# A decoder block's prologue reordered: the second token block's rows loaded ahead of the conditioning weights, and the later sums and low parts given to VectorE

## The chip, the cores and the metric

One core of a Trainium2 chip runs the whole block. The metric is the device time of one execution in microseconds. Engines are named as in the profile: PE (TensorE), DVE (VectorE), ACT (ScalarE), POOL (GpSimd) and SP (SyncE, which here only issues transfers).

## The reference

One layer on a sequence of 2048 tokens, width 1024, all in float32. A vector c gives six vectors of shift, scale and gate; the first two act on the normed tokens, and those go through one input projection:

```python
mod = jax.nn.silu(c) @ w_cond[l] + b_cond[l]
shift_m, scale_m, gate_m, shift_f, scale_f, gate_f = [
    m[:, None, :] for m in jnp.split(mod, N_MOD, axis=-1)]
h = rmsnorm(x, g_mix_pre[l]) * (1.0 + scale_m) + shift_m
proj = h @ w_in[l]
q, k, v, u = jnp.split(proj, [SB_WIDTH, 2 * SB_WIDTH, 3 * SB_WIDTH], axis=-1)
...
attn = stick_breaking_attention(to_heads(q), to_heads(k), to_heads(v))
pool = pooling_mixer(u, w_pool[l], pool_scale[l])
mix = jnp.concatenate([attn, pool], axis=-1) @ w_out[l]
x = x + gate_m * rmsnorm(mix, g_mix_post[l])
```

A SwiGLU feed-forward with its own shift, scale and gate follows. The change is in the prologue: the first two of the six vectors, and the first products of the input projection.

## The kernel before, in words

Every float32 matrix product is made of three products of rounded parts. A tensor is split into a high part (a copy rounded by ACT) and a low part (the tensor minus its high part); `split` (L57) does this, the low part on DVE or, in `chunk_split` (L455), on POOL. `mm3` (L65) multiplies high by high, high by low and low by high.

Tokens go in four blocks of 512 (tb 0 to 3), turned so that the 1024 features lie on partitions in 8 tiles k of 128. The input projection is cut into chunks of 128 columns (q, k, u chunks, each a 512 KB transfer by `chunk_load`, L446). A product of a chunk with a token block is 8 x 3 = 24 matmuls of 128x512.

The order on PE, ACT, DVE and POOL is the order in which the code records them; SP's order is the scheduler's. Eight transfers can be under way at a time: each issue waits for the landing of the eighth before it.

The prologue has to bring together three things before the first product: normed and turned token rows, shift and scale as columns, and a split chunk of w_in. Shift and scale are sums over the 1024 rows of w_cond, weighted with silu(c), 8 steps kc with 128 rows each. They are made in two halves of 512 columns, and each half feeds four of the 8 tiles k:

- Rows of tb 0 are loaded (`row_load`, L555) into `early_hi`, normed (`normed_rows`, L308: square with row sum on ACT, a power on POOL, a scaling on DVE) and turned by PE (`turn_rows`, L573) into `turned`.
- First half: `sums_load` (L585) brings each pair of steps in two 512 KB pieces, one for each part. Part 0 (shift) is summed by DVE into `acc0` (`cond_step`, L214); part 1 (scale) by PE, with one column of weights, into one row, which `row_end` (L603) turns into a column. `sums_end` (L610) turns `acc0` into a column by matmuls with ones, adds the biases, and gives `mods` (held in `sumsq`).
- Then `modulate0` (L638) makes high and low parts of the tokens' tiles 0 to 3, and `first_products` (L654) multiplies three chunks (0, 1 and "third") with them. Rows of tb 1 were loaded into `early_lo`; they are normed and scaled, and `turn1` (L648) turns and modulates their tiles 0 to 3.
- Second half: both parts are summed by DVE, in 512-column steps with two accumulators; `sums_end(1)`, then tiles 4 to 7 of both blocks, and the rest of the first products.
- The fourth chunk ("fourth", u) opens the regular loop (`pieces`, L459, woven with `rest_of_cond`, L294, which sums parts 2 to 5 on DVE). In it `gate_part` (L237) makes the gate's broadcast with two pairs of matmuls into banks of `z_ps`.

PSUM has eight banks, handed out in fixed cycles: `z_ps` (three), `t_ps` (two), `av_ps` (two), `mm_only` (one). Regular products alternate between `z_ps` and `mm_only`.

Of the kernel before, what the change touches and what calls it, by code (L numbers as in the profile page):

```python
# [17 lines left out]
P = 128  # L18
# [26 lines left out]
def block_kernel(ctx, tc, x, c, w_cond, b_cond, g_mix_pre, g_mix_post, w_in, w_pool,  # L45
# [58 lines left out]
    mods["am"], mods["bm"] = sumsq[:, 0:KC], sumsq[:, KC:]  # L104
# [91 lines left out]
    c_sb = cond.tile([P, KC], F32, tag="c", bufs=1, name="c_sb")  # L196
    nc.sync.dma_start(c_sb, c[0].rearrange("(p kc) -> p kc", p=P))
    vrows = cond.tile([P, P], F32, tag="vrows", bufs=1, name="vrows")
    nc.sync.dma_start(vrows[0:48, :], b_cond[0].rearrange("(r q) -> r q", q=P))
    nc.sync.dma_start(vrows[48:56, :], g_mix_pre[0].rearrange("(r q) -> r q", q=P))  # L200
    nc.sync.dma_start(vrows[56:64, :], g_ffn_pre[0].rearrange("(r q) -> r q", q=P))
    nc.sync.dma_start(vrows[64:68, :], pool_scale[0].rearrange("(r q) -> r q", q=P))
    nc.scalar.activation(cs, c_sb, AF.Sigmoid)
    nc.vector.tensor_tensor(cs, cs, c_sb, ALU.mult)
    tv = t_ps("tv")
    nc.tensor.transpose(tv[:, 0:68], vrows[0:68, :], ident[0:68, 0:68])
    nc.vector.tensor_copy(colv, tv[:, 0:68])
# [29 lines left out]
    def gate_part(acc, part, g_post, dst):  # L237
# [7 lines left out]
        for half in range(2):  # L245
            cols = slice(half * TB, (half + 1) * TB)
            ps = z_ps(f"gp{part}_{half}")
            nc.tensor.matmul(ps, ones_r, hi[:, cols], start=True, stop=False)
            nc.tensor.matmul(ps, ones_r, lo[:, cols], start=False, stop=True)
            nc.vector.tensor_tensor(g[:, cols], g[:, cols], ps, ALU.mult)  # L250
# [9 lines left out]

    def cond_sums(part, acc):
        for kc in range(KC):
            while ahead_wc and len(coming_wc) <= 3:
                p, k = ahead_wc.pop(0)
                coming_wc.append(cond_load(p, k, new_wc(f"wc{p}_{k}") if k < 6 else spare[:, k - 6]))
# [42 lines left out]
    def normed_rows(tb, j, xs=None):  # L308
# [11 lines left out]
        if tb == 1:  # L320
            return lambda: nc.scalar.mul(xs, xt, r) if j % 2 else nc.vector.tensor_scalar_mul(xs, xt, r)
# [133 lines left out]
    def chunk_split(c, part):  # L455
        ks = slice(2 * part, 2 * part + 2)
        split(c[1][:, ks, :], c[2][:, ks, :], c[0][:, ks, :], nc.gpsimd)
# [101 lines left out]

    ready = [row_load(0, j) for j in range(4)]  # L560
    for j in range(4):
        normed_rows(0, j, ready[j])
    acc0 = new_acc(0)
    sums = [z_ps("am")]
    row = cond.tile([1, TB], F32, tag="brow", bufs=1, name="am_row")
    acc1 = cond.tile([P, D], F32, tag="acc", bufs=2, name="acc1")
    by_tensor = (tuple(range(KC)), ())
    by_vector = [[kc for kc in range(KC) if kc not in r] for r in by_tensor]
    halves = [slice(half * TB, (half + 1) * TB) for half in range(2)]
# [3 lines left out]
    def turn_rows(j):  # L573
        for half in range(2):
# [5 lines left out]
            if half or j > 1:  # L580
# [4 lines left out]
    def sums_load(half, pair):  # L585
        two = wcs[:, pair]
        wc = cond.tile([P, 2, TB], F32, tag="wc", bufs=4, name=f"wc1_{half}_{pair}")
        nc.sync.dma_start(wc, wc_rows[:, 2 * pair:2 * pair + 2, D + half * TB:D + (half + 1) * TB])
        nc.sync.dma_start(two, wc_rows[:, 2 * pair:2 * pair + 2, halves[half]])
        return two, wc  # L590

    def sums_step(half, pair, two, wc):
        for kk in range(2):
            kc = 2 * pair + kk
            cond_step(acc0[:, halves[half]], kc, two[:, kk])
            if kc in by_vector[half]:
                cond_step(acc1[:, halves[half]], kc, wc[:, kk])
            else:
# [70 lines left out]
    for pair in range(4):  # L669
        turn_rows(pair)  # L670
# [1103 lines left out]
```

## Time and profile before

| | |
|---|---|
| median of 3 runs | 2265.72 us (2265.38 to 2267.29) |
| the profiled execution | 2265.84 us |
| its span | 2264.0 us |
| mean granted PE clock | 0.996 |
| PE busy | 2231.9 us (99%) |
| DVE, ACT, POOL busy | 72%, 52%, 57% |
| first product of the projection starts | 27.07 us |
| fourth chunk's first product starts | 76.41 us |

A row of the profile's order of time has start (us from the span's start), duration, engine, line, operation, output<-inputs, shapes, count of merged instructions, and in brackets the engine's idle time ahead of it with what ended it. A row of the table by stretches of time has the stretch, its length, busy time and count for PE, PEld (weight loads), DVE, ACT and POOL, then the granted clock, the share of the transfer engines, and GB/s. "SPq" is SP issuing a transfer.

### The profile page before, as it was taken

How to read it: one execution, taken by the hardware profiler on the slowest of the kernel's cores; microseconds unless marked ns; L12 is line 12 of the kernel's file. 1: busy time of each engine (PE TensorE's matmuls, PEld its weight loads, DVE VectorE, ACT ScalarE, POOL GpSimd, SP SyncE). 2: the span in 40 equal slices, each digit the busy share in tenths (PEclk: the TensorE clock that was granted, in tenths of full speed). 3: DMA queues.
4: the chain of work that ended last, by engine and by line, in shares of the span. 5: the costliest groups of instructions: out<-in, count | busy, mean ns of one | idle time of the engine just before them, and what ended most of it. 6: DMA issues, size and time to landing. Idle time of an engine off the chain costs nothing.

```text
span 2264.0 us, 33220 instructions
## 1 busy us (share of the span) xinstructions
PE 2231.9 (99%) x10589; PEld 1845.3 (82%) x10589; DVE 1628.4 (72%) x2213; ACT 1167.3 (52%) x2422; POOL 1298.2 (57%) x1606
## 2 busy tenths in 40 slices
PE   7999999999999999999999999999999999999998
PEld 5788888888888878887888888888888888888887
DVE  6884599999999966666656566777866565655566
ACT  5334589989989854453232323455533323334444
POOL 3652267787779955546777777321676665651003
PEclk9999999999999999999999999999999999999999
DMA  8885886634443456665444455777853333328654
GB/s 298 302 298 204 288 213 178 174 91 117 134 112 108 139 189 214 222 219 171 160 160 161 158 163 180 270 242 229 259 174 122 101 112 94 115 88 296 216 189 149
DMA packets 323979, 413.55 MB, mean 183 GB/s; under 512 B 20630, under 2 KB 189146, under 8 KB 323676
## 3 DMA queue, kind: packets, MB, share of 16 engines
q1 hardware_dynamic: 319340, 408.81, 56.2%
q10 hardware_dynamic: 4464, 2.62, 0.4%
q8 instruction: 83, 1.36, 0.3%
q14 instruction: 92, 0.75, 0.1%
HBM read 282.90 MB, written 128.45 MB: 182 GB/s over the span
## 4 chain that ended last, share of the span: by engine, by line
PE 88%; DVE 5%; ACT 3%; issue 2%; DMA 1%; POOL 1%; SPq 0%; DVEq 0%; ACTq 0%; POOLq 0%
PE wt L914 4%; PE t_g L69 3%; PE t_u L69 3%; PE t_g L70 3%; PE t_u L70 3%; PE t_u L71 3%; PE t_g L71 3%; PE dn0p L71 3%; PE dn0p L70 3%; PE dn0p L69 3%; PE dn1p L70 3%; PE dn1p L69 3%; PE dn1p L71 3%; PE b_g L69 3%; PE b_g L70 3%; PE b_g L71 3%
## 5 line engine op out<-in xcount | busy, mean ns | idle before, releaser
L903 POOL TENSOR_TENSOR w<-sg,pr 128x512 f32<-128x512 f32 (+2 forms) x320 | 307.1, 960 | 47.6 <-DVE pr L898 16.1
L1288 POOL TENSOR_TENSOR s<-s,cu 128x512 f32<-128x512 f32 x88 | 133.6, 1525 | 237.5 <-DVE cu L1287 142.6
L898 DVE TENSOR_TENSOR_SCAN pr<-pr,carry,begin 128x512 f32<-128x512 f32 x192 | 243.9, 1270 | 0.0
L882 ACT ACTIVATE sg<-z 128x512 f32<-128x512 f32 (+2 forms) x320 | 183.4, 573 | 50.6 <-PE z L880 40.7
L60 DVE TENSOR_TENSOR wtl<-wt,wth 128x512 fp32r<-128x512 f32 (+1 forms) x320 | 189.2, 592 | 17.9 <-ACT wth L59 16.0
L59 ACT CAST wth<-wt 128x512 fp32r<-128x512 f32 (+1 forms) x320 | 182.1, 571 | 12.1 <-PE wt L914 12.1
L884 ACT ACTIVATE pr<-z 128x512 f32<-128x512 f32 (+2 forms) x320 | 182.5, 570 | 0.0
L914 PE MATMUL wt<-ident,w 128*128 128x128 f32 x1088 | 172.5, 273 | 1.8 <-POOL pr L894 1.1
L60 DVE TENSOR_TENSOR u_s_l<-u_s,u_s_h 128x512 fp32r<-128x512 f32 x66 | 65.2, 988 | 149.9 <-ACT u_s_h L59 149.9
L914 PEld LDWEIGHTS wt<-ident,w 128*128 128x128 f32 x1088 | 134.1, 140 | 33.2 <-POOL pr L894 1.9
L1278 ACT ACTIVATE s<-s 128x512 f32<-128x512 f32 x88 | 55.7, 633 | 184.7 <-DVE s L1277 184.7
L929 PE MATMUL av<-wth,vt 128*128 128x512 f32 (+1 forms) x320 | 126.4, 395 | 0.9 <-ACT o L934 0.8
L60 DVE TENSOR_TENSOR u_a_l<-u,u_a_h 128x512 fp32r<-128x512 f32 x66 | 76.2, 1156 | 63.6 <-ACT u_a_h L59 63.6
L930 PE MATMUL av<-wtl,vt 128*128 128x512 f32 (+1 forms) x320 | 118.1, 369 | 1.9 <-DVE wtl L60 1.7
L69 PE MATMUL dn0p<-w0p_h,g0p_h 128*128 128x512 f32 x308 | 119.8, 389 | 0.0
L70 PE MATMUL dn0p<-w0p_l,g0p_h 128*128 128x512 f32 x308 | 119.8, 389 | 0.0
L71 PE MATMUL dn0p<-w0p_h,g0p_l 128*128 128x512 f32 x308 | 119.8, 389 | 0.0
L879 PE MATMUL z<-kt,qt 128*128 128x512 f32 (+2 forms) x320 | 118.7, 371 | 0.7 <-ACT pr L884 0.6
L59 ACT CAST g_s_h<-g_s 128x512 fp32r<-128x512 f32 x66 | 39.5, 620 | 152.5 <-POOL g_s L1220 77.6
L880 PE MATMUL z<-kt,qt 128*128 128x512 f32 (+2 forms) x320 | 117.0, 366 | 0.0
L59 ACT CAST u_s_h<-u_s 128x512 fp32r<-128x512 f32 x66 | 38.6, 614 | 151.1 <-POOL u_s L1220 149.3
L69 PE MATMUL dn1p<-w1p_h,g1p_h 128*128 128x512 f32 x292 | 113.6, 389 | 0.0
(692 smaller groups left out, 7210.9 us busy)
## 6 DMA issues: line engine op xcount, KB each, us to landing
g<-in_w_gate_dram SPq DMA_DIRECT2D x42, 512.0 KB, 5.5
u<-in_w_up_dram SPq DMA_DIRECT2D x42, 512.0 KB, 4.0
wc<-in_w_cond_dram SPq DMA_DIRECT2D x32, 512.0 KB, 7.3
qt<-qd SPq DMA_DIRECT2D x64, 256.0 KB, 3.9
kt<-kd SPq DMA_DIRECT2D x96, 128.0 KB, 3.4
vt<-vd SPq DMA_DIRECT2D x48, 256.0 KB, 3.6
wd<-in_w_down_dram SPq DMA_DIRECT2D x44, 256.0 KB, 3.0
tdt<-wd SPq DMA_DIRECT2D x44, 256.0 KB, 2.0
```

What stands on the lines that cost most here:

```text
L59: nc.scalar.copy(hi, src)
L60: low.tensor_tensor(lo, src, raw(hi), ALU.subtract)
L69: nc.tensor.matmul(ps, lh, rh, start=first and i == 0, stop=False)
L70: nc.tensor.matmul(ps, lh, rl, start=False, stop=False)
L71: nc.tensor.matmul(ps, ll, rh, start=False, stop=last and i == n - 1)
L882: nc.scalar.activation(sg[:, 0:L], z[:, 0:L], AF.Sigmoid, scale=0.125)
L884: nc.scalar.activation(pr[:, 0:L], z[:, 0:L], AF.Sigmoid, scale=-0.125)
L898: nc.vector.tensor_tensor_scan(keys, keys, begin, carry, ALU.mult, ALU.bypass)
L903: nc.gpsimd.tensor_tensor(w[:, 0:L], sg[:, 0:L], pr[:, 1:L + 1], ALU.mult)
L914: nc.tensor.transpose(wt[:, i * P:(i + 1) * P], wss[u][i][:, b * P:(b + 1) * P], ident)
L929: nc.tensor.matmul(av[:, lo0:], vb, wh[:, lo0:], start=first, stop=False)
L1288: nc.gpsimd.tensor_tensor(s, s, u, ALU.mult)
```

## The change

1. The five small loads (c, biases, gains) are issued by ACT instead of SP. All eight token row loads, of tb 0 and tb 1, come first on SP.
2. w_cond comes in pieces of one step kc with both parts (`piece_load`), 512 KB each, eight for each half. The first chunk's load stands ahead of the last two pieces of the first half.
3. Rows of tb 1 are normed right after those of tb 0, and their tiles 0 to 3 are turned on PE between the row matmuls (`turn_early`) into four PSUM banks, from which `turn1` reads them.
4. The first half's two columns are made together (`columns`, one addition for both). The order of `mods["am"]` and `mods["bm"]` in `sumsq` is exchanged for that.
5. In the second half DVE sums both parts in one step of 1024 columns into one accumulator (`late_sum`).
6. All low parts of the modulated tokens, and those of chunk 1 and the third chunk, are made by DVE. POOL keeps those of chunk 0 and of the fourth chunk.
7. The last six matmuls of the third chunk's first half come after the columns of the second half. The fourth chunk's splits are spread over the products of tiles 4 to 7, its load stands behind loads for part 2.
8. `gate_part` takes its banks from `av_ps` instead of `z_ps`.

```diff
@@ gate_part
-            ps = z_ps(f"gp{part}_{half}")
+            ps = av_ps(f"gp{part}_{half}")
@@ modulate
-        (nc.gpsimd, nc.vector)[kc % 2 or (tb, kc) == (0, 0)].tensor_tensor(lo, h32, raw(hi), ALU.subtract)
+        nc.vector.tensor_tensor(lo, h32, raw(hi), ALU.subtract)
@@ loads
+    def piece_load(half, kc):
+        piece = wcs[:, kc - HK] if kc >= HK else cond.tile([P, 2, TB], F32, tag="wc", bufs=4, name=f"wc1_{half}_{kc}")
+        nc.sync.dma_start(piece, parts01[:, kc, 0:2, halves[half]])
+        return piece
...
     ready = [row_load(0, j) for j in range(4)]
+    nc.scalar.dma_start(c_sb, c[0].rearrange("(p kc) -> p kc", p=P))
...
+    early1 = [row_load(1, j) for j in range(4)]
...
+    coming = [piece_load(0, kc) for kc in range(6)]
+    loaded.append(chunk_load(chunks[0], 0))
+    coming += [piece_load(0, kc) for kc in range(6, KC)]
+    loaded.append(chunk_load(chunks[1], 0))
@@ first half
+    for j in range(4):
+        turn_rows(j)
+        normed_rows(1, j, early1[j])
+        if j:
+            for kc in (2 * j - 2, 2 * j - 1):
+                cond_step(acc[:, 0:TB], kc, coming[kc][:, 0])
...
+    for kc in range(KC):
+        if kc % 2 == 0:
+            turn_early(kc // 2)
+        nc.tensor.matmul(sums[0:1, :], cs[:, kc:kc + 1], coming[kc][:, 1], start=not kc, stop=kc == KC - 1)
+    nc.scalar.copy(row, sums[0:1, :])
+    ps0 = z_ps("am_columns0")
+    columns(ps0, acc[:, 0:TB])
+    columns(ps0, row, HK)
@@ second half
+    def late_sum(kc):
+        cond_step(acc, kc, late_pieces[kc].rearrange("p m n -> p (m n)"))
...
+    first_products(2, 1, 0, 1)
     pt4 = turned1(HK)
-    sums_end(1)
+    ps1 = t_ps("am_columns1")
+    columns(ps1, acc)
+    sums_end(1, ps1)
+    first_products(2, 1, 2, 3)
     modulate0(4, 5)
-    chunk_split(loaded[2], 2)
-    chunk_split(loaded[2], 3)
+    chunk_split(loaded[1], 2, nc.vector)
+    chunk_split(loaded[2], 2, nc.vector)
     modulate0(6, 7)
+    chunk_split(loaded[1], 3, nc.vector)
+    chunk_split(loaded[2], 3, nc.vector)
```

SP's queue in the kernel before, up to the third chunk's load. `early_hi` and `early_lo` are the rows of tb 0 and tb 1, `wc_` and `wcs` pieces of w_cond, `wq`, `wk` chunks of w_in; the second `wq` is the third chunk:

```order
L557 DMA early_hi<-in_x_dram 128x1024 x4
L588 DMA wc_0_0_319<-in_w_cond_dram 128x2x512
L589 DMA wcs<-in_w_cond_dram 128x2x512
...
L588 DMA wc_0_3_328<-in_w_cond_dram 128x2x512
L589 DMA wcs<-in_w_cond_dram 128x2x512
L451 DMA wq_0_32_402<-in_w_in_dram 128x8x128
L451 DMA wk_0_32_406<-in_w_in_dram 128x8x128
L557 DMA early_lo<-in_x_dram 128x1024 x4
L588 DMA wc_1_0_414<-in_w_cond_dram 128x2x512
...
L451 DMA wq_0_32_422<-in_w_in_dram 128x8x128
```

The same queue in the change:

```order
L546 DMA early_hi<-in_x_dram 128x1024 x4
L546 DMA early_lo<-in_x_dram 128x1024 x4
L554 DMA wc_0_0_287<-in_w_cond_dram 128x2x512
...
L554 DMA wcs<-in_w_cond_dram 128x2x512 x2
L440 DMA wq_0_32_297<-in_w_in_dram 128x8x128
L554 DMA wcs<-in_w_cond_dram 128x2x512 x2
L440 DMA wk_0_32_303<-in_w_in_dram 128x8x128
L554 DMA wc_1_0_469<-in_w_cond_dram 128x2x512
...
L554 DMA wc_1_3_479<-in_w_cond_dram 128x2x512
L554 DMA wcs<-in_w_cond_dram 128x2x512
L440 DMA wq_0_32_477<-in_w_in_dram 128x8x128
```

The rows of tb 1 and the first chunk moved ahead of the first half's last pieces, and the third chunk stands behind five pieces of the second half; three more follow it.

DVE between the first late sum and the second columns, in the change (`acc` is the accumulator, `ht1a` the low parts of tb 1's tiles 0 to 3):

```order
L205 TENSOR_SCALAR acc_307<-wc_1_0_469,cs 128x1024
L60 TENSOR_TENSOR thirdl<-wq_0_32_477,thirdh 128x256 x2
L614 TENSOR_TENSOR ht1a<-h_0_546,ht1a 128x512
L614 TENSOR_TENSOR ht1a<-h_1_550,ht1a 128x512
L207 SCALAR_TENSOR_TENSOR acc_307<-wc_1_1_471,cs,acc_307 128x1024
L207 SCALAR_TENSOR_TENSOR acc_307<-wc_1_2_473,cs,acc_307 128x1024
L614 TENSOR_TENSOR ht1a<-h_2_569,ht1a 128x512
L614 TENSOR_TENSOR ht1a<-h_3_573,ht1a 128x512
L207 SCALAR_TENSOR_TENSOR acc_307<-wc_1_3_479,cs,acc_307 128x1024
L207 SCALAR_TENSOR_TENSOR acc_307<-wcs,cs,acc_307 128x1024 x4
L600 TENSOR_TENSOR sumsq<-am_columns_620,colv 128x2x4
```

Before, that stretch had 16 sums of 512 columns and the two odd low parts of `ht1a`; POOL made the even ones and `thirdl`.

PE at the gate's matmuls, before:

```order
L248 MATMUL gp_0_1040<-gs2xt,ones_r 128x512
L249 MATMUL gp_0_1040<-gs2xs,ones_r 128x512 [waits DVE_49]
L248 MATMUL gp_1_1044<-gs2xt,ones_r 128x512 [waits DVE_49]
L249 MATMUL gp_1_1044<-gs2xs,ones_r 128x512
L69 MATMUL u_0_1035<-hth_275,wu_0_h 128x512
```

and in the change:

```order
L236 MATMUL gp_0_1028<-gs2xt,ones_r 128x512
L237 MATMUL gp_0_1028<-gs2xs,ones_r 128x512 [waits DVE_49]
L236 MATMUL gp_1_1032<-gs2xt,ones_r 128x512
L237 MATMUL gp_1_1032<-gs2xs,ones_r 128x512
L69 MATMUL u_0_1023<-hth_263,wu_0_h 128x512
```

The second pair no longer waits for DVE.

189 lines of the change are left out of this document (79 added, 110 removed).

## The prediction

> **What bounds the kernel now.** I read the busy times and the chain first, then TensorE in order of time with the idle time ahead of each row, then the granted clock over the same stretches, and last the engines and transfers that TensorE waits for.
>
> ```profile
> PE 2231.9 (99%) x10589; PEld 1845.3 (82%) x10589; DVE 1628.4 (72%) x2213; ACT 1167.3 (52%) x2422; POOL 1298.2 (57%) x1606
> PE 88%; DVE 5%; ACT 3%; issue 2%; DMA 1%; POOL 1%; SPq 0%; DVEq 0%; ACTq 0%; POOLq 0%
> ```
>
> TensorE is busy for 99% of the span and 88% of the chain that ends last lies on it. So an early delay or gain on TensorE reaches the end one to one. What can be won is its idle time (2264.0 - 2231.9 = 32.1 us in all) and the time at half clock. In TensorE's order of time, seven rows mark the prologue and what follows (start, duration, idle before and what ended it):
>
> ```profile
> 27.07 1.50 PE L661 MATMUL first<-hth,wq_h 128*128 128x512 f32 x2 [1.80 <-ACT hth L631]
> 51.33 1.92 PE L619 MATMUL am_columns<-ones,acc 128*128 128x1 f32 x16
> 54.54 0.49 PE L69 MATMUL first<-hth,wq_h 128*128 128x512 f32 x1 [1.29 <-ACT hth L631]
> 55.94 0.80 PE L70 MATMUL first<-htl,wq_h 128*128 128x512 f32 x1 [0.91 <-POOL htl L636]
> 76.18 0.39 PE L71 MATMUL first<-ht1b,thirdl 128*128 128x512 f32 x1
> 76.41 0.39 PE L69 MATMUL u<-hth,fourthh 128*128 128x512 f32 x1
> 101.19 0.50 PE L248 MATMUL gp<-gs2xt,ones_r 128*128 128x512 f32 x1 [1.72 <-DVE k L60]
> ```
>
> The first product starts at 27.07 us, when the first half of the conditioning sums has become a column. The products of that half last until the second half's columns at 51.33, then 1.29 and 0.91 us of idle follow, and from 55.94 the remaining products run without a gap to 76.41, where the fourth chunk begins. The last row is a wait outside the prologue: the gate's second matmul stands 1.72 us for a PSUM bank that VectorE has not read out. The granted clock (the column before the DMA share):
>
> ```profile
> 27.07:31.31 4.24, 4.24 (x8) 2.28 (x8) 2.95 (x7) 4.24 (x9) 1.73 (x3) 0.50 1.03 395
> 54.54:62.03 7.49, 6.58 (x17) 4.94 (x18) 5.46 (x6) 3.48 (x7) 6.02 (x5) 0.54 0.39 127
> 62.03:76.41 14.38, 14.38 (x68) 11.86 (x67) 9.28 (x12) 6.14 (x12) 5.51 (x5) 1.00 0.82 275
> ```
>
> After each of the two column stages TensorE runs at half clock, the second time for most of 7.5 us. With 55.94 to 62.03 busy at half speed, about 3 us of work is lost there.
>
> **Step 1, the first sums: 4.1 us later.** Rows on the transfers and on what follows the last of them:
>
> ```profile
> 0.74 0.40 SPq L197 DMA_DIRECT2D c_sb<-in_c_dram  x1
> 2.71 1.77 SPq L557 DMA_DIRECT2D early_hi<-in_x_dram  x4
> 6.28 1.06 ACT L317 ACTIVATE xt<-early_hi 128x1024 f32<-128x1024 f32 x1 [3.70 <-DMA early_hi<-in_x_dram]
> 4.50:9.40 4.90, 0.29 (x2) 0.30 (x3) 0.97 (x3) 2.78 (x5) 0.77 (x2) 1.00 1.00 397
> 9.40:20.30 10.90, 10.90 (x44) 6.62 (x43) 7.74 (x13) 5.02 (x10) 1.44 (x3) 1.00 1.04 387
> 20.30:23.90 3.60, 2.94 (x13) 1.22 (x11) 1.50 (x2) 1.60 (x5) 0.58 (x1) 1.00 1.22 305
> 21.10 1.54 DVE L219 SCALAR_TENSOR_TENSOR acc<-wcs,cs,acc 128x512 f32<-128x512 f32 x2 [1.22 <-DMA wcs<-in_w_cond_dram]
> 15.23 7.03 PE L599 MATMUL am<-wc,cs 128*1 128x512 f32 x16
> 22.30 0.57 ACT L601 COPY am_row<-am 1x512 f32<-1x512 f32 x1 [6.27 <-PE am L599]
> 23.32 2.77 POOL L60 TENSOR_TENSOR wq_l<-wq,wq_h 128x256 fp32r<-128x256 f32 x4 [10.62 <-ACT wq_h L59]
> ```
>
> The windows' last number is GB/s: 397 while token rows land (4 KB runs), 387 for w_cond (2 KB), 305 for the w_in chunks wq and wk (512 B). A transfer is 512 KB, 0.524 MB, so 1.32, 1.35 and 1.72 us each. The queue is full from the start, so order decides. Before, four token loads and eight w_cond loads stand ahead of the last piece; the change puts four more token loads and one chunk between, 4 x 1.32 + 1.72 = 7.0 us. SP starts 2.71 - 0.74 = 2.0 us earlier, because five small loads go to ScalarE's queue: its first load then takes the place of the first load of c at 0.74. The last piece lands at 21.1 + 7.0 - 2.0 = 26.1 us. From there to the first product it took 27.07 - 21.10 = 6.0 us. The copy of the row of sums (0.57) now runs beside the accumulator's columns, and TensorE, behind with its 16 row matmuls until 22.26, has only the last pair left (0.3 saved): about 5.1 us. First product: 31.2 us, 4.1 later; bounds +2.5 (SP's earlier start worth nothing) to +5.5. VectorE and ScalarE do eight token rows instead of four before that, but land-to-land spacing (1.32 us) roughly equals their 1.3 to 1.5 us per row, and I put that at nothing: if the cover is gone, each 0.5 us there shows in full.
>
> The Trainium skill ("DMA: Bandwidth & Descriptors", Specifications) gives 512 B as the least run for line rate. The 305 GB/s of the 512-byte chunks speaks against it; by it wq would cost 1.35 us and step 1 would be 0.4 us smaller. I keep the row.
>
> **Step 2, the second sums: they end where they did.** Durations:
>
> ```profile
> 26.22 0.55 DVE L635 TENSOR_SCALAR h<-turned,sumsq 128x512 f32<-128x512 f32 x1
> 27.05 0.69 DVE L636 TENSOR_TENSOR htl<-h,hth 128x512 fp32r<-128x512 f32 x1 [0.29 <-ACT hth L631]
> 36.93 0.71 ACT L59 CAST thirdh<-wq 128x256 fp32r<-128x256 f32 x2
> 37.55 0.77 ACT L631 ACTIVATE ht1a<-x,sumsq 128x512 fp32r<-128x512 f32 x1
> 38.22 0.77 ACT L633 ACTIVATE h<-x,sumsq 128x512 f32<-128x512 f32 x1
> 40.36 1.22 DVE L636 TENSOR_TENSOR ht1a<-h,ht1a 128x512 fp32r<-128x512 f32 x1 [1.16 <-ACT h L633]
> 50.45 0.73 DVE L219 SCALAR_TENSOR_TENSOR acc<-wc,cs,acc 128x512 f32<-128x512 f32 x1
> 81.22 1.27 DVE L219 SCALAR_TENSOR_TENSOR acc<-wc,cs,acc 128x1024 f32<-128x1024 f32 x1
> 106.28 0.74 DVE L217 TENSOR_SCALAR acc<-wc,cs 128x1024 f32<-128x1024 f32 x1
> 164.14 0.41 DVE L60 TENSOR_TENSOR wvl<-spare,wvh 128x256 fp32r<-128x256 f32 x1
> ```
>
> Two limits meet. VectorE: from 30.3, 0.9 us ahead of the first product as before (26.22 to 27.07), it does four pairs h and low part, 4 x (0.55 + 0.69), two low parts of wk at 0.41 and the first late sum at 0.74, which ends at 36.8. Transfers: behind the last piece at 26.1 stand wk, five late pieces and the third chunk, 1.72 + 5 x 1.35 + 1.72 = 10.2 us, so the third chunk lands at 36.3. ScalarE stands in order: two casts of the third chunk (0.71, starting about 36.4), then the four turned tiles, two ops each at 0.67 from start to start; the second tile's h is done at 40.0. Behind that VectorE has one low part 0.69, two late sums, two low parts, five late sums: 0.69 + 2 x 1.27 + 2 x 0.69 + 5 x 1.27 = 11.0 us, end 51.0. Before, the last sum ended at 50.45 + 0.73 = 51.2. With GpSimd quiet I take the lone durations (0.69, not the 1.22 beside GpSimd). So 4.1 us of delay is paid by the products' slack: TensorE has 66 matmuls at 0.23 us (76.18 to 76.41, the pace at full clock) = 15.2 us and about 2.5 us of half clock ahead of the columns, is there at about 49.5 (with four transposes) and waits 1.5 us. Columns end at 52.9 against 51.33 + 1.92 = 53.25: **-0.3 us**. Bounds: +2.5 if step 1 or the chunk comes that much later; -1.5, where TensorE becomes the limit.
>
> **Step 3, after the second columns: -1.3 us.**
>
> ```profile
> 53.75 1.00 DVE L635 TENSOR_SCALAR h<-turned,sumsq 128x512 f32<-128x512 f32 x2
> 54.56 1.32 POOL L636 TENSOR_TENSOR htl<-h,hth 128x512 fp32r<-128x512 f32 x1 [11.16 <-ACT hth L631]
> 60.80 1.05 PE L645 MATMUL x<-ident,early_lo 128*128 128x128 f32 x4
> 64.58 0.60 PE L645 MATMUL x<-ident,early_lo 128*128 128x128 f32 x4
> 64.94 0.48 PE L69 MATMUL first<-hth,wk_h 128*128 128x512 f32 x1
> ```
>
> Six matmuls of the third chunk now stand behind the columns and fill the 1.29 us. The first low part comes from VectorE, h 0.5 us after the columns (53.75 to 53.25) for 0.55, then 0.69 alone, in all 1.75 us; before it was GpSimd's 1.32 and TensorE went on 55.94 - 53.25 = 2.7 us after them: -0.95. Three groups of four transposes remain behind the columns where four stood, one of them at half clock (64.94 - 64.58 = 0.36 for one at full clock): -0.35. The rest of the products is the same. Half clock: waiting 1.5 us, columns 1.9 us, so I expect the same 3 us lost and no change; bounds -3 (no loss) and +0.5 (the six matmuls fall under it too).
>
> The fourth chunk's load now waits for VectorE's last low part of wk, four pairs and three splits after the columns: 53.4 + 4 x 1.24 + 3 x 0.41 = 59.6. With 3.6 us from issue to use (2.71 to 6.28) and a load ahead of it, it lands near 64, and ScalarE holds a cast of it ahead of two turned tiles. TensorE asks for those tiles from about 68 on; with that cover gone, each us later costs one. SP holds the first products' stores behind that load and two more; nobody reads them for long, so I cost that at nothing.
>
> **Step 4, the gate's banks: -1.2 us.**
>
> ```profile
> 104.48 0.68 DVE L60 TENSOR_TENSOR k<-k,k 128x512 fp32r<-128x512 f32 x1
> 106.54 0.39 PE L69 MATMUL u<-ht1a,wu_h 128*128 128x512 f32 x1
> ```
>
> The gate's two matmuls take banks that nobody holds, and the 1.72 us wait goes. What is late next: the following product at 106.54 needs the bank that VectorE frees at 104.48 + 0.68 = 105.2, so only about 1.3 us can be kept, and I take 1.2. Bounds: 0 (the next wait takes all) and -1.8.
>
> Sum: -0.3 - 1.3 - 1.2 = **-2.8 us**. The profiled execution took 2265.84 us (span 2264.0 and 1.84 around it), 0.12 above the median 2265.72. Forecast 2265.8 - 2.8 = **2263.0 us**, on its own 2260.6 to 2265.5.
>
> **Rivals.**
> - *The clock holds.* The six matmuls behind the columns keep TensorE in use, and it does not fall to half clock a second time: 2263.0 - 3.0 = 2260.0. Against: the clock fell before beside pauses of 1.29 and 0.91 us and columns of 1.92; here a wait of 1.5 us and the same columns stand together. For it: six matmuls in the place of the longer pause. The Trainium skill ("TensorE: Matmul & The Clock Gate", Why this matters for your kernels) asks only that pauses stay under about 3 us; by that rule it would hold here, but the trace of before shows 0.54 with pauses of 1.29 us.
> - *The second wait goes as well.* If the third chunk lands 1.5 us earlier, VectorE stands less behind ScalarE, TensorE reaches the columns as they are ready and the weak stretch shrinks to the columns' 1.9 us: 2263.0 - 1.5 - 3.0 = 2258.5. Against: VectorE's other limit lies only 0.5 us ahead.
> - *Slower: the first sums' delay goes through.* One mechanism: transfers. If the third chunk lands 4 us later than 36.3 (the queue is starved because its load waits for GpSimd's low parts of wq, and SP issues in order, holding three late pieces behind it), ScalarE's turned tiles and VectorE's sums move with it, and the columns end at 53.25 + 3.7. Then 2265.8 + 3.7 - 1.3 - 1.2 = 2267.0. It decides from about 36.8 us on, each us there costing one. For it: those low parts take 2.77 us from ScalarE's casts on and end only near 31. Against: the queue still holds 3 us of earlier loads then.
> - *Nothing.* The early half is there, but VectorE, busy for 9.67 of 10 us there (row below), frees the bank no earlier than at 105.2, and the product at 106.54 comes 1.3 us earlier whatever was won ahead of it; with half of that lost again, 2265.2.
>
> ```profile
> 100.00:110.00 10.00, 8.81 (x39) 7.30 (x40) 9.67 (x9) 2.40 (x7) 8.50 (x8) 1.00 0.92 314
> ```
>
> **Chances.** Forecast 0.45, clock holds 0.13, second wait gone 0.14, slower 0.18, nothing 0.10. A measurement here tells about 0.2%, 4.5 us: below 2261.2 lie the two fast cases and a few hundredths of the forecast, less what of them ends above, 0.28; above 2270.3 the longer delays of the slower case, 0.07; 0.65 within. The range runs from 2258.0, a little past the fastest rival, to 2268.5, past the slow one.
>
> **What would show it.** Step 1: last piece waited for near 26 us and first product near 31. Step 2: the third chunk's cast near 36.4, last late sum ending near 51. Step 3: under 2 us from the end of the columns to the first matmul on a low part; fourth chunk's first product near 74.8. Step 4: no wait ahead of the gate's second matmul. It is wrong if w_cond overtakes the token loads, if the clock stays full past 53 us, or if the columns end more than 2 us from 52.9.

## The result, and the profile after

The changed kernel takes 2279.56 us (median of 6 runs, 2278.33 to 2280.63), the kernel before, run beside it, 2267.16 us (6 runs, 2265.38 to 2267.91): a ratio of 1.0056, 95% interval 1.0043 to 1.0069. It is slower by 0.56%. Forecast were 2263.0 us and a range of 2258.0 to 2268.5; the chance of slower by over 0.2% was put at 0.07. The profiled execution took 2278.33 us, with a span of 2276.5 against 2264.0. The same two rows of the page, now of the changed kernel:

```profile
PE 2235.0 (98%) x10589; PEld 1844.5 (81%) x10589; DVE 1627.9 (72%) x2222; ACT 1162.9 (51%) x2418; POOL 1274.3 (56%) x1591
PE 87%; DVE 5%; issue 2%; ACT 2%; DMA 2%; POOL 1%; SPq 0%; ACTq 0%; DVEq 0%; POOLq 0%
```

The work is the same. TensorE is idle for 41.5 us instead of 32.1 (span less busy time) and, with the same matmuls, busy 3.1 us longer. Half clock explains a part of that: up to 100 us the changed kernel is busy for 13.5 us at a granted clock of 0.50, the kernel before for 11.1, which makes about 1.2 us (an estimate, half of the difference); the rest is not taken apart. The order of time of TensorE in the changed kernel:

```profile
17.38 0.33 PE L648 MATMUL x<-ident,early_lo 128*128 128x128 f32 x1 [1.27 <-ACT turned L588]
24.08 0.90 PE L648 MATMUL x<-ident,early_lo 128*128 128x128 f32 x3 [6.37 <-DVE x_v L121]
24.91 3.36 PE L666 MATMUL am<-wc,cs 128*1 128x512 f32 x4
28.80 1.88 PE L666 MATMUL am<-wc,cs 128*1 128x512 f32 x4
33.59 1.88 PE L666 MATMUL am<-wcs,cs 128*1 128x512 f32 x4
35.40 1.05 PE L594 MATMUL am_columns<-ones,acc 128*128 128x1 f32 x8
38.79 1.50 PE L639 MATMUL first<-hth,wq_h 128*128 128x512 f32 x2 [1.36 <-ACT hth L609]
57.88 1.95 PE L594 MATMUL am_columns<-ones,acc 128*128 128x1 f32 x16 [0.30 <-DVE acc L207]
61.92 0.50 PE L70 MATMUL first<-htl,wq_h 128*128 128x512 f32 x1 [0.22 <-DVE htl L614]
67.84 0.63 PE L623 MATMUL x<-ident,early_lo 128*128 128x128 f32 x4 [2.56 <-DVE h L613]
84.48 0.39 PE L69 MATMUL u<-hth,fourthh 128*128 128x512 f32 x1
96.47 0.50 PE L71 MATMUL k<-hth,wk_l 128*128 128x512 f32 x1 [0.43 <-POOL wk_l L60]
101.09 0.50 PE L71 MATMUL k<-hth,wk_l 128*128 128x512 f32 x1 [2.95 <-POOL wk_l L60]
111.72 0.39 PE L236 MATMUL gp<-gs2xt,ones_r 128*128 128x512 f32 x1
116.93 0.39 PE L69 MATMUL u<-ht1a,wu_h 128*128 128x512 f32 x1
```

The reader is to see a wait of 6.37 us in the second row, long before any product, and the sixteen row matmuls (L666) queued behind it: they begin at 24.91 though the first piece of w_cond is there since 15.8 (the trace's landing time). The first product is 11.72 us late. From place to place, start of the same matmul before and after:

| place | before | after | shift |
|---|---|---|---|
| first product | 27.07 | 38.79 | +11.72 |
| second columns | 51.33 | 57.88 | +6.55 |
| fourth chunk's first product | 76.41 | 84.48 | +8.07 |
| first product of k with block 1 | 92.73 | 105.14 | +12.41 |
| u behind the gate | 106.54 | 116.93 | +10.39 |
| end of the span | 2264.0 | 2276.5 | +12.5 |

So 11.72 us are lost ahead of the first product, 5.17 won back up to the second columns, 1.52 lost behind them, 4.34 lost between the fourth chunk and k, 2.02 won at the gate, and 2.1 lost behind it.

VectorE in the changed kernel, in order of time, around the end of TensorE's wait:

```profile
21.22 0.75 DVE L311 TENSOR_SCALAR early_lo<-early_lo,x_r 128x1024 f32<-128x1024 f32 x1 [0.73 <-POOL x_r L123]
21.89 1.53 DVE L207 SCALAR_TENSOR_TENSOR acc<-wc,cs,acc 128x512 f32<-128x512 f32 x2
23.34 0.68 DVE L590 COPY turned<-x_pt 128x512 f32<-128x512 f32 x1
25.48 3.11 DVE L207 SCALAR_TENSOR_TENSOR acc<-wcs,cs,acc 128x512 f32<-128x512 f32 x4
```

The third row is what TensorE waited for: the copy of the last turned tile out of its PSUM bank. TensorE had filled that bank by 16.1; VectorE, in order, first normed the rows of block 1 and summed w_cond. The early transposes take the same bank again (`t_ps` and the cycle of `turn_rows` share it). The releaser that the profile names, x_v, is only VectorE's next instruction. ScalarE, SP and GpSimd in the changed kernel, one fence each:

```profile
35.98 1.32 ACT L59 CAST wq_h<-wq 128x256 fp32r<-128x256 f32 x4
43.51 0.71 ACT L59 CAST thirdh<-wq 128x256 fp32r<-128x256 f32 x2 [2.06 <-DMA wq<-in_w_in_dram]
84.57 0.59 ACT L59 CAST q<-first 128x512 fp32r<-128x512 f32 x1 [7.11 <-DMA qd<-q]
```

```profile
39.44 0.37 SPq L440 DMA_DIRECT2D wq<-in_w_in_dram  x1
66.66 0.38 SPq L440 DMA_DIRECT2D wu<-in_w_in_dram  x1
78.79 0.38 SPq L440 DMA_DIRECT2D wu<-in_w_in_dram  x1
79.27 0.53 SPq L357 DMA_DIRECT2D qd<-q  x1
```

```profile
36.46 2.96 POOL L60 TENSOR_TENSOR wq_l<-wq,wq_h 128x256 fp32r<-128x256 f32 x4 [11.69 <-ACT wq_h L59]
77.24 1.52 POOL L60 TENSOR_TENSOR fourthl<-wu,fourthh 128x256 fp32r<-128x256 f32 x2 [3.26 <-ACT fourthh L59]
96.38 3.97 POOL L264 TENSOR_TENSOR spare<-spare 128x1024 f32<-128x1024 f32 x1
```

The third chunk (in the buffer wq) is issued at 39.44, when GpSimd has read the first chunk. The next load of wu waits until 78.76 for GpSimd's low parts of the fourth chunk, and the first store of q stands behind it on SP. ScalarE waits 7.11 us for that store before it casts q again, VectorE's sums of part 2 follow, and GpSimd's addition of 3.97 us then falls ahead of the low part of wk for which TensorE waits 2.95 us.

The granted clock in the changed kernel (the column before the share of the transfer engines):

```profile
21.10:27.94 6.84, 3.86 (x7) 0.84 (x7) 5.85 (x10) 0.00 (x0) 0.63 (x2) 0.50 1.10 335
38.20:45.00 6.80, 6.21 (x14) 4.40 (x15) 6.38 (x12) 4.74 (x10) 1.22 (x2) 0.50 0.65 211
57.88:68.90 11.02, 7.94 (x41) 5.94 (x42) 7.77 (x16) 5.22 (x10) 0.00 (x0) 1.00 0.18 54
68.90:72.30 3.40, 3.40 (x12) 2.71 (x11) 1.50 (x2) 0.90 (x3) 0.03 (x1) 0.50 1.00 316
```

Half clock now stands behind the 6.37 us wait, behind the first columns and behind the 2.56 us wait, but no longer behind the second columns.

### The profile page after: what moved, and what is told of

Same layout as the page of the kernel before. It is cut to its first block, busy times and chain, and to the rows that moved or that the text cites. A ratio compares the mean times of both kernels' runs of the same rounds, so it can differ in the third digit from the quotient of the medians.

```text
span 2276.5 us, 33213 instructions
## 1 busy us (share of the span) xinstructions
PE 2235.0 (98%) x10589; PEld 1844.5 (81%) x10589; DVE 1627.9 (72%) x2222; ACT 1162.9 (51%) x2418; POOL 1274.3 (56%) x1591
## 4 chain that ended last, share of the span: by engine, by line
PE 87%; DVE 5%; issue 2%; ACT 2%; DMA 2%; POOL 1%; SPq 0%; ACTq 0%; DVEq 0%; POOLq 0%
PE wt L917 4%; PE t_g L69 3%; PE t_u L71 3%; PE t_g L70 3%; PE t_u L69 3%; PE t_u L70 3%; PE t_g L71 3%; PE dn0p L70 3%; PE dn0p L71 3%; PE dn0p L69 3%; PE dn1p L69 3%; PE dn1p L70 3%; PE dn1p L71 3%; PE b_u L69 3%; PE b_u L71 3%; PE b_g L71 3%
## 5 line engine op out<-in xcount | busy, mean ns | idle before, releaser
L906 POOL TENSOR_TENSOR w<-sg,pr 128x512 f32<-128x512 f32 (+2 forms) x320 | 306.5, 958 | 46.6 <-DVE pr L901 15.8
```

Of the source, the lines that this page charges most:

```text
L906: nc.gpsimd.tensor_tensor(w[:, 0:L], sg[:, 0:L], pr[:, 1:L + 1], ALU.mult)
```

## The experiments

Theory A, from these rows: TensorE, in order, stands for a bank that VectorE reads out late; that sets the first sums, and the order of a load ahead of the stores and a second bank add the rest. Rival B: transfers set the first sums. Rival C: VectorE's order and its added work, with GpSimd quiet, cost the time.

**The last copy to ScalarE.** In `turn_rows`:

```diff
-            if half:
+            if half or j == 3:
                 nc.scalar.copy(dst, src)
```

> The changed kernel, but the last of VectorE's four copies of turned token rows (x_3, half 0) goes to ScalarE. In the trace of the changed kernel that copy ran at 23.34 us and TensorE's second early transpose, which needs its bank, stood 6.37 us until 24.08, the 16 row matmuls behind it. Theory A (TensorE, in order, stands for a bank that VectorE reads out late, and this sets the first sums): the row matmuls begin near 20 instead of 24.9, the last ends near 28.5, which the last piece's landing at 27.1 sets, the first product starts at 31 to 32.5 instead of 38.79, and of these 6 to 7 us most reach the end: 2272 to 2275 against 2279. Rival B (transfers: the last piece at 27.1 and the third chunk at 43.5 set it): the stand goes, the first product comes at most 1 us earlier, time within 1.5 us of the changed kernel's. Rival C (VectorE's order and its added work set it): VectorE has one copy of 0.68 less, so about 0.7 us is won.

Measured: 2273.19 us against 2266.74, ratio 1.0028 (1.0017 to 1.0040). TensorE in order of time:

```profile
17.60 0.66 PE L648 MATMUL x<-ident,early_lo 128*128 128x128 f32 x4 [1.76 <-ACT turned L588]
18.19 1.88 PE L666 MATMUL am<-wc,cs 128*1 128x512 f32 x4
28.15 1.02 PE L666 MATMUL am<-wcs,cs 128*1 128x512 f32 x2 [0.37 <-DMA wcs<-in_w_cond_dram]
32.55 1.50 PE L639 MATMUL first<-hth,wq_h 128*128 128x512 f32 x2 [1.42 <-ACT hth L609]
```

One copy of 0.68 us on another engine moves the first product by 6.24 us. Only now does TensorE wait for the last piece. A holds for the first stage: B allowed at most 1 us there, C about 0.7.

**The row matmuls ahead of the early transposes.**

```diff
     for kc in range(KC):
-        if kc % 2 == 0:
-            turn_early(kc // 2)
         nc.tensor.matmul(sums[0:1, :], ...
...
     columns(ps0, row, HK)
+    for j in range(4):
+        turn_early(j)
```

> The changed kernel, but all 16 row matmuls and the columns stand ahead of the early transposes on TensorE; every copy stays on its engine. Theory A: nothing stands ahead of the row matmuls, they end near 28.5 (last piece at 27.1), the first product starts at 31 to 33 instead of 38.79 (16 transposes now lie between the columns and it, in part beside VectorE's and ScalarE's work), time 2272 to 2275. Rival B: as for the first experiment, within 1.5 us of the changed kernel. Rival C: VectorE's order is unchanged, so no gain.

Measured: 2271.73 us, ratio 1.0023 (1.0013 to 1.0034); first product at 32.49. VectorE's work and its order are the same as in the changed kernel, so the stand itself was the cost. TensorE further on:

```profile
27.86 1.02 PE L664 MATMUL am<-wcs,cs 128*1 128x512 f32 x2 [0.37 <-DMA wcs<-in_w_cond_dram]
51.28 2.05 PE L594 MATMUL am_columns<-ones,acc 128*128 128x1 f32 x16 [1.66 <-DVE acc L207]
```

The second columns begin at 51.28, after a wait of 1.66 us. The third chunk is issued at 32.87, when GpSimd ends its last low part of the first chunk (32.85), and lands at 36.88 (the trace's landing time).

**The order behind the second columns as before.**

```diff
-    load_ahead()
     loaded.append(chunk_load(chunks[3], 0, ...))
...
-    turn1(4, pt4)
-    first_products(0, 0, 4, 5)
-    ...
+    for ks in ((4, 5), (6, 7)):
+        for n in range(3):
+            first_products(n, 0, *ks)
+            if n < 2:
+                turn1(ks[n], pt4 if ks[n] == HK else None)
+            run_small()
```

(with the fourth chunk's splits back among the products of block 1).

> The changed kernel, but the part behind the second columns (order of the products, turned tiles, small tasks and the fourth chunk's splits, and the load of w_cond ahead of the fourth chunk's) as in the kernel before. In the changed kernel's trace a load that waits for GpSimd until 78.8 stood on SP ahead of the first products' stores, ScalarE's casts that wait for those stores came 14 us later, and products of k waited 0.43 + 2.95 us, with 4.34 us lost from the fourth chunk to there. Theory A with this as its second place: those waits go, time 3 to 4.5 us less: 2275 to 2276.5. Rival: the casts are late because the whole prologue is 8 us late; then 1 us or less is won.

Measured: 2275.78 us, ratio 1.0041 (1.0028 to 1.0054). From the fourth chunk's first product to k with block 1 it takes 83.70 to 100.03 = 16.33 us; before 16.32, changed 20.66. No wait ahead of k is left. On SP the first store goes out with no load of wu ahead of it that waits for GpSimd:

```profile
69.83 0.42 SPq L230 DMA_DIRECT2D spare<-in_g_ffn_post_dram  x1
75.50 0.38 SPq L357 DMA_DIRECT2D qd<-q  x1
```

All 4.34 us come from this part of the change. The edit puts back the order of products, turned tiles and splits together with the load; that the load ahead of the store is the cause within it is read from the rows, and was not changed alone.

**The gate's banks alone, in the kernel before.**

```diff
-            ps = z_ps(f"gp{part}_{half}")
+            ps = av_ps(f"gp{part}_{half}")
```

> The kernel before, with the gate's two matmuls on the other pair of banks and nothing else changed. The prediction's step 4 says -1.2 us (bounds 0 and -1.8). The changed kernel's trace shows 2.0 us won at that place: -2.0. The rival of the prediction (the bank of the next product takes all of it): 0 to -0.3. Time near 2265, which by itself can hardly be told from 2267; the trace shows it by the wait ahead of the gate's second matmul and by the time of the next product.

Measured: 2264.99 us against 2266.74, ratio 0.9992 (0.9983 to 1.0001). The wait ahead of the gate's second matmul is gone, and the next product has one instead:

```profile
105.49 0.50 PE L69 MATMUL u<-ht1a,wu_h 128*128 128x512 f32 x1 [0.75 <-DVE k L60]
```

From the gate to there it takes 98.91 to 105.49 = 6.58 us against 98.85 to 106.54 = 7.69: 1.11 won, where 1.2 was predicted. The time alone does not tell it, since its interval reaches 1.0001; the two places do.

**Three mended at once.** The edits of the second and third experiment, and

```diff
-    pt4 = turned1(HK)
     ps1 = t_ps("am_columns1")
+    pt4 = turned1(HK)
```

> Three edits of the changed kernel at once: the row matmuls and columns ahead of the early transposes on TensorE (as in the second experiment), the part behind the second columns as before (as in the third), and the second columns take their bank ahead of the turned tiles of k-tile 4, so that tile 5 does not get a bank that VectorE still reads (2.28 us of wait in the second experiment). If the three losses are separate, as theory A has it, their sum holds: 2271.7 - 4.3 - 2.3 = 2265.1, between 2263.5 and 2266.5, below the kernel before (2266.7). Rival: a wait taken away comes back at the next place (tile 6 then waits for a bank in place of tile 5): 2267 to 2268.

Measured: 2267.88 us against 2266.33, ratio 1.0005 (0.9996 to 1.0014): of the 12.4 us by which the changed kernel is slower, 10.8 are gone; the expectation was 2.8 us lower. The three losses are not separate: the time lies in the rival's range, 2267 to 2268, though the wait comes back at another place than the rival named. TensorE's order shows no wait any more between the second columns (50.83) and the fourth chunk (73.46): 22.63 us, before 25.08. At the fourth chunk the kernel is 2.95 us ahead of before (73.46 to 76.41), at k with block 1 only 0.8 (91.92 to 92.73). In between TensorE waits for a low part of wk; the row shows 1.16 of the 2.1 us that go there:

```profile
87.84 0.50 PE L71 MATMUL k<-hth,wk_l 128*128 128x512 f32 x1 [1.16 <-POOL wk_l L60]
```

GpSimd makes that low part no earlier than before, though TensorE comes 2.95 us earlier; the kernel before first, then this one:

```profile
86.38 1.18 POOL L60 TENSOR_TENSOR wk_l<-wk,wk_h 128x256 fp32r<-128x256 f32 x1
```

```profile
87.07 0.72 POOL L60 TENSOR_TENSOR wk_l<-wk,wk_h 128x256 fp32r<-128x256 f32 x1
```

It ends at 87.56 and 87.79. So the place at which the third experiment showed no wait has one again as soon as TensorE comes early enough. At the gate's second half the lead is 2.7 us, 1.9 of it won at the gate. Then two more waits take most of it back:

```profile
115.27 0.50 PE L69 MATMUL q<-ht1a,wq_h 128*128 128x512 f32 x1 [0.52 <-ACT u L376]
127.29 0.50 PE L71 MATMUL u<-hth,wu_l 128*128 128x512 f32 x1 [1.27 <-POOL wu_l L60]
```

The rest of the lead goes in fractions of a us after 340 us.

**Pieces ahead, small vectors later.** On top of the three edits:

```diff
-    coming = [piece_load(0, kc) for kc in range(6)]
+    coming = [piece_load(0, kc) for kc in range(KC)]
     loaded.append(chunk_load(chunks[0], 0))
-    coming += [piece_load(0, kc) for kc in range(6, KC)]
```

and `tv` with its copy to `colv` behind the loop of `turn_rows`.

> The fifth experiment's kernel, with the first w_in chunk loaded behind all eight early pieces of w_cond instead of ahead of the last two, and with the turning of the small vectors (matmul and VectorE's copy, which in the changed kernel held VectorE's first norm until 8.36 us) moved behind the token rows. Theory A with transfers as the next limit: last piece at 26.1 instead of 27.8, first product at 30.5 to 31.5 instead of 32.5, of which the products' slack ahead of the second columns takes some: 0.5 to 1.5 us below the fifth experiment. Rival (the late sums, behind the third chunk and ScalarE, set the second columns): first product earlier, second columns unmoved at 51 to 51.5, time equal to the fifth experiment's within 0.5.

Measured: 2270.70 us, ratio 1.0019 (1.0010 to 1.0028), slower than without these two edits; both theories missed. The last piece lands at 25.7, 0.7 us earlier than in the kernel with the three edits alone (26.4), but:

```profile
22.59 0.37 PE L655 MATMUL tv<-ident,vrows 68*128 68x68 f32 x1 [8.85 <-DVE x_v L121]
36.22 0.91 PE L635 MATMUL first<-hth,wq_h 128*128 128x512 f32 x2
```

The matmul that I moved takes the bank of the last turned tile and stands 8.85 us for VectorE's copy, the row matmuls behind it. It is the same mechanism, made anew by mistake, and the first product comes 3.6 us later (36.22 against 32.65) although the last piece is there earlier.

**Low parts back to GpSimd**, in the changed kernel: `chunk_split` of chunks 1 and third without `nc.vector`, and in `modulate` the line of before.

> The changed kernel, but with the low parts back where they were before: the splits of the second and third chunk on GpSimd, and the low parts of the turned tiles alternating between GpSimd and VectorE. Rival C (VectorE's added work and GpSimd's quiet cost the time): 2 us or more faster than the changed kernel, 2277 or less. Theory A: the first sums come as late as in the changed kernel (first product at 38 to 39); behind them GpSimd's low parts take 1.3 us against 0.7, so 0 to 2 us slower: 2279 to 2281.5.

Measured: 2279.91 us, ratio 1.0060 (1.0047 to 1.0072), level with the changed kernel. The first product stays at 38.69; the second columns come 1.18 us later, at 59.06, and two late sums take 3.63 us beside GpSimd where they took 2.60. Rival C falls for the changed kernel: the low parts on VectorE were no loss there. Without the stand this was not run.

**The small loads back on SP**, in the changed kernel: `nc.sync.dma_start` for the five, ahead of the token rows.

> The changed kernel, but with the five small loads back at the head of SP's queue, as before. Rival B (transfers set the first sums): every piece lands 2 us later and the time grows by 1.5 to 2 us, to about 2281. Theory A: the small vectors are turned earlier (the column of scales at 4.3 instead of 8.21), VectorE's first norm starts at 7.5 instead of 8.36 behind the first token row, and the stand for VectorE's copy moves with it: first product within 1 us of 38.8, time 2278 to 2280.

Measured: 2278.82 us, ratio 1.0052 (1.0039 to 1.0066), within A's range, though the first product moved a little more than expected, to 37.34. The last piece lands at 27.83 instead of 27.14, but that tells nothing of the small loads: in the eleven traces that have them on ScalarE and the same order of the early loads, it lands between 26.4 and 28.2. On VectorE:

```profile
4.25 0.23 DVE L570 COPY colv<-tv 128x68 f32<-128x68 f32 x1 [1.42 <-PE tv L569]
7.25 0.15 DVE L121 TENSOR_SCALAR x_v<-ss 128x1 f32<-128x1 f32 x1 [2.77 <-ACT xt L308]
```

The first norm starts at 7.25 instead of 8.36, and the copy that TensorE waits for comes 1.1 us earlier.

**Loads earlier.** Four kernels on top of the three edits asked where the lead goes after 100 us. The first casts the first chunk ahead of the copy of the row of sums (`chunk_split(loaded[0], part)` ahead of `nc.scalar.copy(row, ...)`), the second splits parts 2 and 3 of wk ahead of the late sums, the third does both, the fourth also loads all eight pieces ahead of the first chunk.

> The fifth experiment's kernel, with the splits of the first w_in chunk (ScalarE's casts, GpSimd's low parts) ahead of ScalarE's copy of the row of sums instead of behind it. In the fifth experiment the third chunk's load waits for those low parts until 32.51 us and the transfer queue runs dry. Theory D (a load that waits for a buffer starves the queue, and the time comes back as late transfers up to 130 us): the load is issued at 28 to 29.5, lands near 33 instead of 36.4, late sums end 0 to 0.8 earlier; the fourth chunk's load (59.88) still waits, so most of the loss after 100 us stays: 2267 to 2268 against 2267.9. Rival (the first stage sets the time): nothing moves.

> The fifth experiment's kernel, with the last two splits of the second w_in chunk (wk) ahead of the late sums, in place of behind the second columns as in the changed kernel. Theory D: the fourth chunk's load, which waits for that chunk's buffer until 59.88 us (37.15 before the change) and stands on SP ahead of the first stores, is issued near 38 and lands by 50; the queue, at 5 GB/s from 50 to 60 us, is used; the stores of q and k land some us earlier, and the waits at 115.3 (0.52) and 127.3 (1.27), where the won 2.1 us shrink to 0.6, go: 1.5 to 2.5 us less, 2265.5 to 2266.5, though VectorE has 0.84 us more ahead of the second columns (50.83 becomes 51 to 51.7). Rival (VectorE's and GpSimd's own work sets those waits): only the 0.84 shows, 2268 to 2268.7.

> The edits of the two experiments before together. Theory D: third chunk lands near 33, which pays VectorE's 0.84 us of extra splits, second columns at 50.5 to 51, fourth chunk's load issued before 38: 2 to 3 us less than the fifth experiment, 2265 to 2266, which is below the kernel before by 0.5 to 1.5. Rival: as in the tenth, no gain, 2267.5 to 2268.5.

> The eleventh experiment's kernel, with the first w_in chunk loaded behind all eight early pieces of w_cond: one half of the sixth experiment, without the move of the small vectors, which there put a matmul ahead of the row matmuls that stood 8.85 us for a bank of VectorE's. Theory A: the sixth experiment was slow by that stand alone; here the last piece lands at 26.1, the row matmuls end near 27.3, VectorE's early sums near 28, first product 0.5 to 1 us earlier than in the eleventh, and the time 0 to 1 us less than there. Rival (the order of the loads made the sixth slow, since the first chunk's casts and the third chunk's load come later): 1 to 3 us slower than the eleventh.

| | us | beside before | ratio, 95% interval |
|---|---|---|---|
| first | 2266.60 | 2266.44 | 1.0002 (0.9992 to 1.0011) |
| second | 2267.38 | 2266.44 | 1.0005 (0.9996 to 1.0014) |
| third | 2267.64 | 2266.44 | 1.0004 (0.9995 to 1.0013) |
| fourth | 2266.45 | 2266.44 | 0.9999 (0.9990 to 1.0008) |

None differs from before, or from the three edits alone, by more than its interval. The loads do move (the third chunk's is issued at 29.6 in the first, the fourth's at 40.3 in the second). But in the first and third kernel the early casts bring GpSimd's low parts beside VectorE's early sums, whose last four then take 4.61 us where they take 3.21 in the second, and TensorE waits 1.59 and 0.43 us for them. One row of each, the first kernel first:

```profile
25.50 4.61 DVE L207 SCALAR_TENSOR_TENSOR acc<-wcs,cs,acc 128x512 f32<-128x512 f32 x4
```

```profile
25.32 3.21 DVE L207 SCALAR_TENSOR_TENSOR acc<-wcs,cs,acc 128x512 f32<-128x512 f32 x4
```

In the fourth kernel GpSimd starts only at 27.83 and the four sums take 3.11 us. The last piece is there at 25.5, but VectorE sums until 28.4, and TensorE waits for it all the same:

```profile
28.53 1.64 PE L593 MATMUL am_columns<-ones,acc 128*128 128x1 f32 x8 [2.01 <-DVE acc L207]
```

Theory D, that a starved queue alone gives the lead back, is not borne out: the two kernels for which it gave 1.5 to 3 us, the second and third, came out level. The fourth run does tell one thing of the sixth experiment: the same order of loads, with the early splits and without the moved small vectors, is not slow, so its 8.85 us stand was the cause.

**Two loads less, five loads less**, on the three edits: the load of part 4's k-tiles left out as the expectations say.

> The fifth experiment's kernel, with two loads of w_cond left out (part 4, k-tiles 1 and 2: the sums of these two steps take the piece of k-tile 0 again, so the gate of the second half is computed from other numbers); every engine does the same work. It asks what takes back, between 115 and 128 us, the 2.1 to 2.7 us by which the fifth experiment is ahead of the kernel before at 100 us. Theory E (transfers: the queue stands at 0.93 to 1.06 from 80 us on, and the load of wu lands at 118.6 whatever TensorE won before): wu lands about 2.6 us earlier, at 116, the waits ahead of q at 115.3 (0.52) and of u at 127.3 (1.27) go, and the time is 1.3 to 2.5 us less than 2267.9: 2265.4 to 2266.6. Rival (VectorE's and GpSimd's order sets those waits): wu lands earlier, but the waits keep at least 1.2 of their 1.8 us, and the time stays at 2267 to 2268.5.

> As the thirteenth experiment, but five loads of w_cond left out (part 4, k-tiles 1 to 5, whose sums take the piece of k-tile 0 again; every engine does the same work), 5 x 1.3 = 6.5 us of transfers. The thirteenth's time (2265.7 beside 2265.8 of before) lay in the range of theory E, but its trace had a pause of 2.01 us ahead of k and half clock behind it, so that TensorE had nothing to give back at 115. Theory E (transfers take the lead back): the time is at least as low as with two loads less and at most 2 us lower, 2263.5 to 2265.7, TensorE keeps what lead it has at 105 us until 130 us, and wu lands 5 us or more ahead of the product that uses it. Rival (VectorE's and GpSimd's order): time 2266.5 to 2268.5 and a loss of 1 us or more of the lead between 105 and 130 us.

Measured: 2265.72 us against 2265.84 with two less (0.9999, 0.9990 to 1.0008), and 2273.46 against 2266.28 with five less (1.0032, 1.0020 to 1.0045). The first lies where transfers would put it, but its interval overlaps that of the three edits, and its trace does not decide: the waits at 115 and 127 are absent, yet TensorE comes there 3.6 us later than in the kernel with three edits (q with block 1 at 118.89 against 115.27), after a pause of 2.01 us ahead of k, and wu lands at 118.8 where the theory said 116. The second is spoilt by the edit: the order of the loads that remain changes, and ScalarE stands for one of them, TensorE 6.59 us with it:

```profile
108.71 1.15 ACT L262 ACTIVATE spare<-spare,cs 128x1024 f32<-128x1024 f32 x1 [10.68 <-DMA spare<-in_w_cond_dram]
```

What takes the lead back between 115 and 128 us, transfers or the order of VectorE and GpSimd, stays open.

## Why the prediction was wrong, point by point

**Step 1 failed, and with it the forecast.** It put the first product at 31.2 from "TensorE, behind with its 16 row matmuls until 22.26, has only the last pair left". The last piece came at 27.14 (26.1 predicted), and at that time TensorE was at the third of sixteen. The working counted transfers, copies and columns, but gave the early transposes no wait of their own: nobody asked which PSUM banks they take, who reads those, and where that reader stands in its order. It said of VectorE's four added token rows "if the cover is gone, each 0.5 us there shows in full"; the cover that went was the bank's copy behind two norms and four sums. With the stand taken away the first product comes at 32.55 and 32.49 in the first two experiments, 1.3 above the step's value and at the edge of its bounds (+5.5 is 32.57); in four other kernels with the same order up to there it comes at 32.65, 33.99, 34.12 and 36.44, each with a stretch of half clock ahead of it. A second term was mis-sized, SP's earlier start, put at 2.0 us. The last piece comes at 27.81 in the second experiment, 1.7 later than predicted; with the small loads on ScalarE it comes between 26.4 and 28.2, with them on SP at 27.83, so no gain shows. The fourth row load waited until 4.82 for c's landing. The prediction counted "SP's earlier start worth nothing" as its lower bound, +2.5; by its own sum that case is 4.1 + 2.0 = +6.1, above its upper bound.

**Step 2 came out under its own condition, in part by luck.** With the first product at 32.5, the third chunk lands at 36.88 (36.3 predicted), TensorE waits 1.66 us (1.5) and the second columns start at 51.28 (51.0). But the chunk's time was worked out from 10.2 us of transfers in the queue ahead of it; in the run its load was issued only at 32.87, when GpSimd had read the first chunk, and landed 4.0 us later. That is the condition of the slower rival, and that the two times agree is luck. In the changed kernel all of it is shifted by step 1: the chunk at 43.49, because GpSimd's low parts wait for ScalarE's casts, which stand behind the copy of the row of sums.

**Step 3: the sign was wrong.** Predicted -1.3, measured +1.52 (8.07 - 6.55). The part that it worked out was better than predicted: with the second columns' bank taken first and the old order behind them, 22.63 us against 25.08, -2.45. The largest things that it left out were tile 5's bank, a wait of 2.56 us for VectorE's h of tile 4, and 1.7 us of half clock behind it (3.40 x 0.5); the rest is not taken apart. "SP holds the first products' stores behind that load and two more; nobody reads them for long, so I cost that at nothing" was the other false term: ScalarE waits for these stores before it casts again, and 4.34 us went (shown for this part of the change as a whole, read from the rows for the stores). The place was seen and the reader was not looked for.

**Step 4 was right.** 1.11 alone for 1.2. In the changed kernel it is 2.02, past the bound of 1.8, since the product behind the gate no longer waits there.

**The rivals.** The slower one named the starved third chunk, 4 us late, with step 1 intact; the chunk came 7.2 us late, but as a result of the stand. Its mechanism was at work (the load did wait for GpSimd's low parts) and was not the cause. The clock did hold behind the second columns (1.00 from 57.88), with a wait of 0.30 us. By the Trainium skill ("TensorE: Matmul & The Clock Gate", Why this matters for your kernels) it should hold as well with waits up to about 3 us; where the second columns waited 1.28 us, in the kernel with three edits, it did not: 0.80 granted over 53 to 60 us. Over the changed kernel and its variants, the clock held behind the second columns where these had waited up to 0.77 us and fell to 0.50 for 3.4 us or more where they had waited 0.94 to 1.69. The measurement decides.

## What to carry to other kernels

Before work is put early on an in-order engine, name for each of its instructions the buffer it writes, the last reader of that buffer, and that reader's place in its own order; everything behind the instruction inherits that wait. A store costs nothing only if nobody waits for its buffer: look for the next writer, not for the next reader. When such a stand is mended, a gain ahead of a stage that keeps several engines and the transfers full may not reach the end: here 2.95 us at 73 us were 0.8 at 92, and 2.7 at 100 us became nothing by 2265. A wait that is absent while TensorE is late can come back once it is early.

## What the runs showed that I had not expected

- Five small loads on ScalarE's queue, beside token rows on SP's, land late: c, issued at 0.73, lands at 4.81; alone ahead of the rows, issued at 0.74, at 2.40. The Trainium skill ("DMA: Bandwidth & Descriptors", Issuing engines are not separate DMA queues) says that a second issuing engine saves only the time of issuing. The traces agree in that no more is won: of the 2.0 us of issuing that SP was spared, no gain shows in the landing of the last piece.
- The clock scatters from run to run in the prologue. After the wait of 2.1 us for the seventh piece, ahead of the same row matmuls, the granted clock from 28 to 36 us was 1.00 in the second experiment and 0.50 in the kernel with wk split early, whose first product then came at 36.44 instead of 32.49. One row of each, the second experiment first:

```profile
28.00:36.00 8.00, 7.41 (x45) 5.58 (x44) 5.40 (x10) 5.33 (x11) 2.98 (x4) 1.00 0.83 277
```

```profile
28.00:36.00 8.00, 8.00 (x32) 6.44 (x31) 2.83 (x7) 4.18 (x9) 2.77 (x4) 0.50 0.72 244
```
